# Second mixer's attention: key-by-query scores, row maxima from rounded products, division after the values

## The chip, the cores and the metric

One core of one Trainium2 chip runs the whole program in one launch. The metric is the device time of one execution in microseconds (us); three runs of the kernel before are shown, and one more execution was recorded by the profiler. Engines: TensorE (PE; its weight loads are PEld), VectorE (DVE), ScalarE (ACT), GpSimd (POOL) and SyncE (SP, here the queue that issues weight loads). Each engine works through its own list of instructions in order.

## The reference, cut to what matters

The program is a two-layer network. Layer 0 has a gated linear-attention mixer, layer 1 latent attention (the second mixer), and each layer ends in a mixture of 32 experts. The change lies in the attention of the second mixer: 16 heads, 256 queries, 512 keys (256 of the context, 256 of the sequence), 96 columns of which 32 are rotated, values of 64 columns.

```python
def softmax_attend(q, k, v):
    s = jnp.einsum('bqhd,bkhd->bhqk', q, k).astype(jnp.float32) * (MLA_QK ** -0.5)
    p = jax.nn.softmax(s, axis=-1).astype(v.dtype)
    return jnp.einsum('bhqk,bkhd->bqhd', p, v)
```

q and k are normed over their 96 columns and rotated before; the result goes through an output projection, and then to the router and the second mixture of experts.

## The kernel before, in words

`run` calls the stages in turn: `hgrn`, `moe`, `mla`, `moe`. `mla` (from line 1407 on) is the second mixer. It first projects the four token tiles (lines 1441 to 1486), and then works on four groups of four heads.

`prep(g)` (lines 1504 to 1554) makes one group ready: products for the queries (line 1512), their sum of squares (1518), inverse root (`rstd`), scaling (1520) and rotation (`rope`, 1494 to 1499), eight transposes into qT (1526); products for keys and values (1534), values copied out (1536), key sum (1541), key scaling (1544), the four rotated parts (1547), sixteen transposes into kT (1553, 1554).

`attend(g)` (lines 1557 to 1584) takes heads in pairs. For a head and each of two query tiles: a product of 128 queries by 512 keys (1567), row maximum (1569), exponential with its row sum (1572), reciprocal and scaling (1573, 1574), four transposes (1577) and a copy (1578) into PT. Then the values are multiplied (1581), and the result is split in a rounded part oH and a rest oL (1583, 1584).

The program calls `prep(0)`, and then for g = 0 to 3 `prep(g + 1)` and `attend(g)`. The adaptive weights of the layer are computed in between (`ada_piece`, line 229 on TensorE, 239 on VectorE), and GpSimd multiplies the output weights by a row of them (line 1611). In this stage a scheduler sets each engine's order when the program is built; it follows the program's text and what its model holds ready.

Two kinds of buffers tie the order down. PSUM tiles come in the order of the text out of rotations: `self.mm()` has four buffers, `self.sm()` two here. And tags with one buffer (q, sqt, kk) let a group in only when the group before has let go.

The weights of the second mixture of experts are loaded ahead by the SyncE queue into nine slots of 2 MB in the order 0, 5, 6, 2, 1, 7, 3, 4, 8 (`wload`, lines 1170 and 1173). During the mixer slot 0 holds scratch tiles, 1 the keys kTs, 2 the query weights wq, 3 and 4 the output weights, 5 wi, and 6 wkv, the weights for keys and values; a load waits until its slot is free, and those behind it wait too.

## Time and profile before

| what | value |
|---|---|
| median of three runs (lowest, highest) | 1554.08 us (1552.7, 1554.46) |
| the profiled execution, its own time | 1554.54 us |
| its span on the core | 1552.9 us |
| granted TensorE clock, mean | 0.985 of full |
| TensorE busy (matmuls) | 1474.2 us, 95% |
| VectorE busy | 808.1 us, 52% |
| ScalarE busy | 441.3 us, 28% |
| GpSimd busy | 48.9 us, 3% |
| read from memory | 498.91 MB, 322 GB/s over the span |

The busy shares are means over stages with different limits, and ends of matmuls are modelled, so 95% does not say that TensorE bounds every stage. The second mixer runs from about 894 to 1075 us of the span; its last value product ends at 1057.6. Matmuls on fp32 tiles are two instructions each in the trace (two passes), transposes and products of rounded (fp32r) tiles are one. Times in rows count from the start of the span.

### The profile page before, as it was taken

What the parts mean: (1) busy time and instruction counts of PE and PEld (TensorE: products, weight loads), DVE (VectorE), ACT (ScalarE), POOL (GpSimd) and SP (SyncE); (2) the same over time, 40 slices, a digit from 0 to 9 for tenths busy, and PEclk for the clock granted to TensorE, in tenths of its full rate; (3) what the DMA queues carried; (4) which work ended last, traced back from release to release, by engine and by line L of the source; (5) the groups of instructions that cost most, each with busy time, mean ns of one, the idle gap of its engine ahead of it and who ended that gap; (6) DMA issues with size and microseconds to landing.
All of it is one profiled execution on the core that took longest, in us unless ns stands there. A gap on an engine that the chain in (4) does not pass through costs nothing. (4 is left out here: it accounts for less than half of the span.)

```text
span 1552.9 us, 20333 instructions
## 1 busy us (share of the span) xinstructions
PE 1474.2 (95%) x8137; PEld 808.7 (52%) x8138; DVE 808.1 (52%) x1651; ACT 441.3 (28%) x937; POOL 48.9 (3%) x81
## 2 busy tenths in 40 slices
PE   7999999999799999999999988989899999999997
PEld 4677777877544444444444454447444443443433
DVE  5686748886625455355355648574333332332333
ACT  4554545663301101111011055564211111111110
POOL 0000000000000000000000103210000000000000
PEclk9999999999899999999999999999999999999999
DMA  9644444126799999999999775355799999999997
GB/s 384 272 179 179 164 189 149 62 109 232 279 364 414 429 426 428 427 427 427 428 428 422 252 301 225 137 190 204 266 417 428 427 428 428 427 428 427 428 424 263
DMA packets 63432, 501.46 MB, mean 323 GB/s; under 512 B 7008, under 2 KB 16608, under 8 KB 33120
## 3 DMA queue, kind: packets, MB, share of 16 engines
q1 hardware_dynamic: 59296, 490.87, 77.6%
q10 hardware_dynamic: 3184, 7.92, 1.5%
q0 software_dynamic: 848, 1.26, 0.3%
q8 instruction: 68, 1.11, 0.3%
q14 instruction: 36, 0.29, 0.1%
HBM read 498.91 MB, written 1.11 MB: 322 GB/s over the span
## 5 line engine op out<-in xcount | busy, mean ns | idle before, releaser
L1179 PE MATMUL mm<-w,xT 128*64 128x512 f32 x2048 | 476.8, 602 | 13.5 <-DMA w<-in_wg_dram 10.0
L1179 PEld LDWEIGHTS mm<-w,xT 128*64 128x64 f32 x2048 | 148.4, 138 | 309.6 <-issue 271.7
L1230 DVE TENSOR_TENSOR tmp<-p,rG 128x512 f32<-128x512 f32 (+1 forms) x106 | 68.0, 645 | 132.7 <-PE p L1228 132.6
L1231 DVE TENSOR_TENSOR x<-x,tmp 128x512 f32<-128x512 f32 (+1 forms) x195 | 132.5, 679 | 6.7
L1230 DVE TENSOR_TENSOR tmp<-p,x 128x512 f32<-128x512 f32 (+1 forms) x68 | 44.5, 655 | 166.3 <-PE p L1228 166.3
L1210 PE MATMUL mm<-w,x 128*64 128x512 f32 (+1 forms) x544 | 115.3, 570 | 1.4 <-ACT x L1198 1.4
L1210 PE MATMUL mm<-w,hT 128*64 128x512 f32 (+1 forms) x544 | 113.9, 570 | 1.4 <-ACT hT L1198 1.4
L560 PE MATMUL mm<-hH,wH 128*128 128x512 f32 x256 | 105.1, 410 | 0.3 <-ACT wH L289 0.3
L1029 PE MATMUL p<-sel,h2H 128*128 128x256 f32 x384 | 101.7, 300 | 2.5 <-DVE sel L1019 2.3
L562 PE MATMUL mm<-hH,wL 128*128 128x512 f32 x256 | 100.3, 392 | 0.5 <-DVE wL L291 0.5
L561 PE MATMUL mm<-hL,wH 128*128 128x512 f32 x256 | 100.0, 391 | 0.0
L1030 PE MATMUL p<-sel,h2L 128*128 128x256 f32 x384 | 98.7, 291 | 0.0
L1217 DVE SCALAR_TENSOR_TENSOR yL<-mm,wsl,yH 128x512 fp32r<-128x512 f32 (+1 forms) x68 | 48.7, 716 | 70.3 <-ACT yH L1216 70.3
L1216 ACT ACTIVATE yH<-mm,wsl 128x512 fp32r<-128x512 f32 (+1 forms) x68 | 45.1, 663 | 122.1 <-PE mm L1210 92.0
L1029 PEld LDWEIGHTS p<-sel,h2H 128*128 128x128 f32 x384 | 76.4, 200 | 5.2 <-issue 4.1
L289 ACT CAST wH<-w 128x1024 fp32r<-128x1024 f32 x55 | 57.3, 1047 | 75.7 <-PE mm L561 56.5
L1030 PEld LDWEIGHTS p<-sel,h2L 128*128 128x128 f32 x384 | 76.3, 199 | 3.1 <-DVE nblki L1098 0.8
L1227 PE MATMUL p<-yH,G 128*128 128x512 f32 (+1 forms) x174 | 76.1, 440 | 0.9 <-DVE tmp L1230 0.9
L291 DVE TENSOR_TENSOR wL<-w,wH 128x1024 fp32r<-128x1024 f32 x55 | 66.8, 1220 | 18.6 <-ACT wH L289 18.1
L1210 PEld LDWEIGHTS mm<-w,x 128*64 128x64 f32 x544 | 45.4, 137 | 58.8 <-issue 45.5
L1210 PEld LDWEIGHTS mm<-w,hT 128*64 128x64 f32 x544 | 37.5, 137 | 65.8 <-issue 59.7
L1227 PEld LDWEIGHTS p<-yH,G 128*128 128x128 f32 x174 | 32.5, 187 | 65.8 <-issue 51.5
(401 smaller groups left out, 2029.1 us busy)
## 6 DMA issues: line engine op xcount, KB each, us to landing
w<-in_wg_dram SPq DMA_DIRECT2D x52, 2048.0 KB, 16.8
w<-in_wu_dram SPq DMA_DIRECT2D x52, 2048.0 KB, 19.7
w<-in_wd_dram SPq DMA_DIRECT2D x52, 2048.0 KB, 18.7
aw<-in_ada_w_dram SPq DMA_DIRECT2D x32, 1024.0 KB, 6.5
w<-in_wd_dram SPq DMA_DIRECT2D x48, 512.0 KB, 8.8
w<-in_hg_w_dram SPq DMA_DIRECT2D x8, 2048.0 KB, 9.2
w<-in_wg_dram SPq DMA_DIRECT2D x32, 512.0 KB, 6.9
w<-in_wu_dram SPq DMA_DIRECT2D x32, 512.0 KB, 9.3
```

What stands on the lines that cost most here:

```text
L289: nc.scalar.copy(H, raw)
L291: nc.vector.tensor_tensor(L, raw, H, op=ALU.subtract)
L560: PE.matmul(p, H[:, c], hH[:, k, :], start=(k == 0), stop=False)
L561: PE.matmul(p, H[:, c], hL[:, k, :], start=False, stop=False)
L562: PE.matmul(p, L[:, c], hH[:, k, :], start=False, stop=(k == 7))
L1029: self.nc.tensor.matmul(o, self.h2H[:, tt, c], r, start=(tt == 0 and k == 0), stop=False)
L1030: self.nc.tensor.matmul(o, self.h2L[:, tt, c], r, start=False, stop=(last and k == 1))
L1179: PE.matmul(p[a * 64:(a + 1) * 64, :], xT[:, k, a * 64:(a + 1) * 64], ws[a][:, k * 512:(k + 1) * 512], start=(k == 0), stop=(k == 7))
L1210: PE.matmul(p[a * 64:(a + 1) * 64, :], hT[:, j, a * 64:(a + 1) * 64], ws[a][:, j * 1024 + n * w_:j * 1024 + n * w_ + w_], start=(j == 0), ...
L1227: PE.matmul(pc, g, yH, start=True, stop=False)
L1230: V.tensor_tensor(t, pc, rG[vec(tt)][:, ns], op=ALU.mult)
L1231: adder.tensor_tensor(x[:, tt, ns], x[:, tt, ns], t, op=ALU.add)
```

## The change

In `prep`, every query and key transpose is also copied into a rounded tile (qR, kR), eight rounded products give the scores of the group once, and their negated row maxima go into a 97th column of q. q is transposed a second time with that column into qT of 97 rows; kT gets a 97th row of ones, so that a product of kT and qT is a score less its row's maximum. In `attend`, scores are computed with keys on the partitions and queries in the columns, the exponential writes PT directly, the sums over keys are two additions on VectorE and a product with ones, and the mixed values are divided at the end. es, rs and on lie in the free end of wkv (slot 6). c becomes a part of one tile cc, in the place that kR takes later. The rest of the program is as before; behind the first edit line numbers are higher by 7 to 22.

```diff
@@ -1438,6 +1438,13 @@
             ckT = wq[:, 3584:4096]
             kg = ar.tile([128, 4, 32], F32, tag="kg", name="kg")
             skr = ar.tile([128, 4], F32, tag="skr", name="skr")
+            G.memset(kTs[96:97], 1.0)
+            cc = ar.tile([128, 4, 512], F32, tag="kR", name="cc")
+            ones = ar.tile([128, 64], F32, tag="on64", name="ones")
+            V.memset(ones, 1.0)
+
+            es = [wkv[:, c:c + 512] for c in (2496, 3008)]
+            rs, on = wkv[:, 3520:3776], wkv[:, 3776:4032]
             for tt in range(4):
                 v = 0 if tt >= 2 else 1
                 ts = slice(tt * 128, tt * 128 + 128)
@@ -1451,7 +1458,7 @@
                         self.scale(k, hT[:, tt % 2, kk, :], pt[:, k * 128:(k + 1) * 128], self.colA[1][:, kk, v:v + 1])
                 if tt == 0:
                     bw = self.mla_bias(ar)
-                jk = ar.tile([128, 4, 256], F32, tag="PT", name="jk", bufs=4)
+                jk = ar.tile([128, 4, 256], F32, tag="PT", name="jk", bufs=3)
                 S.activation(jk.rearrange("p a b -> p (a b)"), y, AF.Square, accum_out=ss[:, tt:tt + 1])
                 if tt == 0:
                     tc.keep_in_program_order(S.preload_act_table_set(TABLE))
@@ -1460,7 +1467,7 @@
                 p = self.mm()
                 for k in range(8):
                     PE.matmul(p[:, c0:416], hT[:, tt % 2, k, :], wi[:, k, c0:416], start=(k == 0), stop=(k == 7))
-                c = ar.tile([128, 512], F32, tag="pr", name="c", bufs=3)
+                c = cc[:, tt, :]
                 V.scalar_tensor_tensor(c[:, c0:416], p[:, c0:416], rx, bw[v], op0=ALU.mult, op1=ALU.add)
                 s2 = self.sp.tile([128, 2], F32, tag="s2", name="s2", bufs=4)
                 jk = ar.tile([128, 1024], F32, tag="q", name="jk")
@@ -1503,7 +1510,8 @@
 
             def prep(g):
 
-                q = ar.tile([128, 1024], F32, tag="q", name="q")[:, 0:768].rearrange("p (h e) -> p h e", h=8)
+                q = ar.tile([128, 1024], F32, tag="q", name="q")[:, 0:776].rearrange("p (h e) -> p h e", h=8)
+                q0 = q[:, :, 0:96]
                 sqt = ar.tile([128, 16, 64], F32, tag="sqt", name="sqt")
                 q2 = sqt.rearrange("p a b -> p (a b)")[:, 0:768].rearrange("p (h e) -> p h e", h=8)
                 for t in range(2):
@@ -1513,18 +1521,12 @@
                                   wq[:, k * 1536 + g * 384:k * 1536 + g * 384 + 384], start=(k == 0), stop=(k == 1))
                     pv = p[:, 0:384].rearrange("p (h e) -> p h e", h=4)
                     S.activation(q2[:, t * 4:t * 4 + 4, :], pv, AF.Square)
-                    V.tensor_tensor(q[:, t * 4:t * 4 + 4, :], pv, gq.to_broadcast([128, 4, 96]), op=ALU.mult)
+                    V.tensor_tensor(q0[:, t * 4:t * 4 + 4, :], pv, gq.to_broadcast([128, 4, 96]), op=ALU.mult)
                 sq = ar.tile([128, 8, 1], F32, tag="sq", name="sq")
                 V.tensor_reduce(sq, q2, axis=AX.X, op=ALU.add)
                 rq = self.rstd(sq[:, :, 0], 96, 8, "rsq")
-                V.tensor_tensor(q, q, rq.rearrange("p (h o) -> p h o", o=1).to_broadcast([128, 8, 96]), op=ALU.mult)
+                V.tensor_tensor(q0, q0, rq.rearrange("p (h o) -> p h o", o=1).to_broadcast([128, 8, 96]), op=ALU.mult)
                 rope(q[:, :, 64:96], cs, 8)
-                qT = ar.tile([96, 4, 256], F32, tag="qT", name="qT", bufs=2)
-                for t in range(2):
-                    pt = self.sm()
-                    for j in range(4):
-                        PE.transpose(pt[0:96, j * 128:(j + 1) * 128], q[:, t * 4 + j, :], self.ident)
-                    S.copy(qT[:, :, t * 128:(t + 1) * 128], pt[0:96].rearrange("p (j t) -> p j t", j=4))
 
                 kk = ar.tile([128, 2048], F32, tag="kk", name="kk")[:, 0:1536].rearrange("p (t h e) -> p t h e", t=4, h=4)
                 sqt = ar.tile([128, 16, 64], F32, tag="sqt", name="sqt")
@@ -1546,42 +1548,62 @@
                 for tt in range(4):
                     V.tensor_tensor(kk[:, tt, :, 64:96], rk[:, tt * 4:tt * 4 + 4].rearrange("p (h o) -> p h o", o=1).to_broadcast([128, 4, 32]),
                                     kg[:, tt:tt + 1, :].to_broadcast([128, 4, 32]), op=ALU.mult)
-                kT = kTs[0:96, g % 2]
+
+                qR = ar.tile([96, 4, 256], F32R, tag="sqt", name="qR")
+                for t in range(2):
+                    pt = self.sm()
+                    for j in range(4):
+                        PE.transpose(pt[0:96, j * 128:(j + 1) * 128], q[:, t * 4 + j, 0:96], self.ident)
+                    S.copy(qR[:, :, t * 128:(t + 1) * 128], pt[0:96].rearrange("p (j t) -> p j t", j=4))
+                kT = kTs[0:97, g % 2]
+                kR = ar.tile([96, 4, 512], F32R, tag="kR", name="kR")
                 for j in range(4):
                     pt = self.sm()
                     for tt in range(4):
                         PE.transpose(pt[0:96, tt * 128:(tt + 1) * 128], kk[:, tt, j, :], self.ident)
-                    S.copy(kT[:, j, :], pt[0:96])
+                    S.copy(kR[:, j, :], pt[0:96])
+                    S.copy(kT[0:96, j, :], pt[0:96])
+                    for t in range(2):
+                        p = self.mm()
+                        PE.matmul(p, qR[:, j, t * 128:(t + 1) * 128], kR[:, j, :], start=True, stop=True)
+                        V.tensor_reduce(q[:, t * 4 + j, 96:97], p, axis=AX.X, op=ALU.max, negate=True)
+                qT = ar.tile([97, 4, 256], F32, tag="qT", name="qT", bufs=2)
+                for t in range(2):
+                    pt = self.sm()
+                    for j in range(4):
+                        PE.transpose(pt[0:97, j * 128:(j + 1) * 128], q[:, t * 4 + j, :], self.ident)
+                    S.copy(qT[:, :, t * 128:(t + 1) * 128], pt[0:97].rearrange("p (j t) -> p j t", j=4))
                 return qT, kT, vS
 
             def attend(g, qT, kT, vS):
+
+
                 for j in range(2):
                     po = self.ac()
                     PTs = []
                     for hh in range(2):
                         h = 2 * j + hh
-                        PT = ar.tile([128, 4, 256], F32, tag="PT", name="PT", bufs=4)
+                        PT = ar.tile([128, 4, 256], F32, tag="PT", name="PT", bufs=3)
                         PTs.append(PT)
-                        for t in range(2):
+                        for b in range(2):
                             p = self.mm()
-                            PE.matmul(p, qT[:, h, t * 128:(t + 1) * 128], kT[:, h, :], start=True, stop=True)
-                            nm = ar.tile([128, 1], F32, tag="nm", name="nm", bufs=8)
-                            V.tensor_reduce(nm, p, axis=AX.X, op=ALU.max, negate=True)
-                            pr = ar.tile([128, 512], F32, tag="pr", name="pr", bufs=3)
-                            sm = ar.tile([128, 1], F32, tag="smx", name="smx", bufs=8)
-                            S.activation(pr, p, AF.Exp, bias=nm, accum_out=sm)
-                            V.reciprocal(sm, sm)
-                            V.tensor_scalar(pr, pr, sm, None, op0=ALU.mult)
-                            pt = self.sm()
-                            for c in range(4):
-                                PE.transpose(pt[:, c * 128:(c + 1) * 128], pr[:, c * 128:(c + 1) * 128], self.ident)
-                            S.copy(PT[:, :, t * 128:(t + 1) * 128], pt.rearrange("p (c q) -> p c q", c=4))
+                            for c in range(2):
+                                s = (2 * b + c) * 128
+                                PE.matmul(p[:, c * 256:(c + 1) * 256], kT[:, h, s:s + 128], qT[:, h, :], start=True, stop=True)
+                            S.activation(PT[:, 2 * b:2 * b + 2, :].rearrange("p c t -> p (c t)"), p, AF.Exp)
+                        V.tensor_tensor(es[hh], PT[:, 0:2, :].rearrange("p c t -> p (c t)"),
+                                        PT[:, 2:4, :].rearrange("p c t -> p (c t)"), op=ALU.add)
+                        V.tensor_tensor(es[hh][:, 0:256], es[hh][:, 0:256], es[hh][:, 256:512], op=ALU.add)
                     for c in range(4):
                         for hh in range(2):
                             PE.matmul(po[hh * 64:(hh + 1) * 64, 0:256], vS[:, c, 2 * j + hh, :], PTs[hh][:, c, :], start=(c == 0), stop=(c == 3))
+                    for hh in range(2):
+                        PE.matmul(po[hh * 64:(hh + 1) * 64, 256:512], ones, es[hh][:, 0:256], start=True, stop=True)
+                    V.reciprocal(rs, po[:, 256:512])
+                    V.tensor_tensor(on, po[:, 0:256], rs, op=ALU.mult)
                     o = g * 2 + j
-                    S.copy(oH[:, o, :], po[:, 0:256])
-                    V.tensor_tensor(oL[:, o, :], po[:, 0:256], oH[:, o, :], op=ALU.subtract)
+                    S.copy(oH[:, o, :], on)
+                    V.tensor_tensor(oL[:, o, :], on, oH[:, o, :], op=ALU.subtract)
 
 
             half = lambda t: [t[:, 0:2048], t[:, 2048:4096]]

```

On TensorE, at the end of attend(0) and in prep(2), the order before was this (L1534: products for keys and values; L1567: scores of attend(1); L229: adaptive weights; L1526, L1553: transposes of queries and keys).

```order
L1534 MATMUL mm<-w_3967,w_3959 128x512 x4
L1567 MATMUL mm<-w_113,qT 128x512 x4
L229 MATMUL p_8133<-w_3966,cS 32x512 x4
L1526 MATMUL p_7857<-ident,q 96x128 x4
L1526 MATMUL p_7863<-ident,q 96x128 x4
L1567 MATMUL mm<-w_113,qT 128x512
L229 MATMUL p_8133<-w_3966,cS 32x512 x3
L229 MATMUL p_8133<-w_112,cS 32x512
L1567 MATMUL mm<-w_113,qT 128x512 x2
L1553 MATMUL p_7908<-ident,kk 96x128 x4
L1553 MATMUL p_7914<-ident,kk 96x128 x4
```

After the change the same place begins with the products with ones of attend(0) (L1601); L1520, L1536, L1556 are the former L1512, L1534, L1526.

```order
L1601 MATMUL p_7800<-w_3967,ones 64x256 x2
L1520 MATMUL mm<-w_3959 128x384 x4
L1536 MATMUL mm<-w_3967,w_3959 128x512 x4
L229 MATMUL p_8115<-w_3966,cS 32x512 x7
L229 MATMUL p_8115<-w_112,cS 32x512 x4
L1556 MATMUL p_7908<-ident,q 96x128 x4
L1556 MATMUL p_7914<-ident,q 96x128 x4
```

And some rows on, at the end of prep(2), with the rounded products (L1568), the second transposes of the queries (L1574) and the first scores of attend(1) (L1592):

```order
L1563 MATMUL p_7960<-ident,kk 96x128 x4
L1568 MATMUL mm<-kR,qR 128x512 x2
L1574 MATMUL p_7974<-ident,q 97x128 x2
L1568 MATMUL mm<-kR,qR 128x512 x2
L1574 MATMUL p_7980<-ident,q 97x128 x2
L1574 MATMUL p_7974<-ident,q 97x128
L1592 MATMUL mm<-qT,w_113 128x256 x2
L1574 MATMUL p_7980<-ident,q 97x128
L1592 MATMUL mm<-qT,w_113 128x256
```

Scores of attend(1) stood ahead of the transposes of prep(2), and stand now behind its rounded products and among its last transposes.

On VectorE, at the end of the rotation of group 0, before (L1499 rotation, L1542 key sum, L1518 sum of squares of group 1):

```order
L1498 TENSOR_TENSOR q<-q,rp_7489 128x8x2x8
L1499 TENSOR_TENSOR q<-q,rp_7488 128x8x2x8
L1542 TENSOR_TENSOR sk<-sk,skr 128x16
L1518 TENSOR_REDUCE sq<-sqt 128x8
L166 TENSOR_SCALAR rsm<-sk 128x16
```

After (L1506 and L1544 are the former L1499 and L1542; L239 is the sum for the adaptive weights):

```order
L1505 TENSOR_TENSOR q<-q,rp_7489 128x8x2x8
L1506 TENSOR_TENSOR q<-q,rp_7488 128x8x2x8
L1544 TENSOR_TENSOR sk<-sk,skr 128x16
L239 TENSOR_TENSOR w_112<-p_8061,w_112 128x512
L166 TENSOR_SCALAR rsm<-sk 128x16
L171 TENSOR_TENSOR rsm<-rsm,rsr 128x16
```

The sum of line 239 stood 26 instructions further on, behind work of group 1, and no work of group 1 stands here now.

On the SyncE queue, the loads for the second mixture of experts, before (w_3966 is slot 5, w_112 slot 0, w_3967 slot 6, w_3959 slot 2, w_3964 and w_3965 slots 3 and 4, w_113 slot 1):

```order
L1170 DMA w_3966<-in_wg_dram 128x4096
L1170 DMA w_112<-in_wg_dram 128x4096
L1170 DMA w_3967<-in_wu_dram 128x4096
L1170 DMA w_3959<-in_wu_dram 128x4096
L1173 DMA w_3964<-in_wg_dram 128x1024 x2
L1170 DMA w_113<-in_wd_dram 128x4096
L1173 DMA w_3964<-in_wg_dram 128x1024 x2
L1173 DMA w_3965<-in_wg_dram 128x1024 x4
```

After:

```order
L1170 DMA w_3966<-in_wg_dram 128x4096
L1170 DMA w_3959<-in_wu_dram 128x4096
L1170 DMA w_112<-in_wg_dram 128x4096
L1173 DMA w_3964<-in_wg_dram 128x1024 x2
L1170 DMA w_113<-in_wd_dram 128x4096
L1170 DMA w_3967<-in_wu_dram 128x4096
L1173 DMA w_3965<-in_wg_dram 128x1024 x2
```

The load into slot 6 went from the third place to behind the load into slot 1, which waits for the last scores.

## Rows read from the trace of the kernel before

**Rows 1.** Stretches: us, busy (x) per engine, TensorE clock, transfer share, GB/s.
```profile
945.00:1057.60 112.60, 102.55 (x516) 52.34 (x514) 74.24 (x176) 62.78 (x155) 28.83 (x19) 0.98 0.49 184
...
1057.60:1094.00 36.40, 29.41 (x156) 25.14 (x156) 22.33 (x66) 15.22 (x30) 1.75 (x7) 0.87 0.63 216
...
1122.00:1300.00 178.00, 175.32 (x834) 74.30 (x830) 61.41 (x108) 29.06 (x54) 0.00 (x0) 0.99 1.01 423
```

**Rows 2.** SyncE's weight queue, waits 890 to 1200: us in total, times, longest.
```profile
SPq L1170 <- PE mm L1179: 27.5, 4, 9.2
...
SPq L1170 <- PE mm L1567: 20.0, 1, 20.0
```

**Rows 3.** Chain of waits in the mixer: start us, us, engine, line, count.
```profile
931.14 2.58 PE mm L1512 x8
...
935.44 0.87 PE p L1526 x8
...
978.78 3.44 PE mm L1567 x8
...
1030.76 3.03 PE p L1581 x14
...
1055.75 1.87 PE p L1581 x14
...
1061.29 0.93 PE mm L1630 x4
```

**Rows 4.** Groups by shape, 919 to 1060: count, busy us, mean ns, idle before.
```profile
L1574 DVE TENSOR_SCALAR pr<-pr,smx 128x512 f32<-128x512 f32 x32 | 25.7, 812 | 1.5
...
L1569 DVE TENSOR_REDUCE nm<-mm 128x1 f32<-128x512 f32 x32 | 21.5, 682 | 3.0 <-PE mm L1567 2.8
...
L1572 ACT ACTIVATE pr<-mm,nm 128x512 f32<-128x512 f32 x32 | 22.1, 695 | 3.5 <-DVE nm L1569 3.3
...
L1554 ACT COPY w<-p 96x512 f32<-96x512 f32 x16 | 8.5, 583 | 9.4 <-PE p L1553 5.5 <-DMA w<-in_ada_b_dram 3.9
...
L1573 DVE RECIPROCAL smx<-smx 128x1 f32<-128x1 f32 x32 | 4.8, 156 | 15.6 <-ACT pr L1572 15.6
```

**Rows 5.** Groups, whole span, VectorE, same columns.
```profile
L391 DVE RECIPROCAL mx<-mx 128x16 f32<-128x16 f32 x1 | 0.3, 252 | 0.0
```

**Rows 6.** Order of time, VectorE, preparation of group 0: start us, us, instruction.
```profile
928.74 0.94 DVE L1518 TENSOR_REDUCE sq<-sqt 128x8 f32<-128x768 f32 x1
...
934.72 0.17 DVE L1542 TENSOR_TENSOR sk<-sk,skr 128x16 f32<-128x16 f32 x1
...
937.66 1.21 DVE L1544 TENSOR_TENSOR kk<-kk,rsr 128x1024 f32<-128x1024 f32 x1
...
938.80 0.89 DVE L1547 TENSOR_TENSOR kk<-rsr,kg 128x128 f32<-128x128 f32 x4
```

**Rows 7.** Order of time, ScalarE and its queue.
```profile
945.00 0.33 ACTq L233 DMA_DIRECT2D w<-in_ada_b_dram  x1
...
952.97 0.58 ACT L1554 COPY w<-p 96x512 f32<-96x512 f32 x1 [3.90 <-DMA w<-in_ada_b_dram]
```

**Rows 8.** Order of time, VectorE and GpSimd (POOL).
```profile
890.11 0.72 DVE L1231 TENSOR_TENSOR x<-x,tmp 128x256 f32<-128x256 f32 x1
...
891.20 0.43 DVE L1231 TENSOR_TENSOR x<-x,tmp 128x256 f32<-128x256 f32 x1
...
944.00 0.69 DVE L239 TENSOR_TENSOR w<-p,w 128x512 f32<-128x512 f32 x1
...
957.84 19.45 POOL L1611 TENSOR_TENSOR w<-w,x 128x1024 f32<-128x1024 f32 x8 [4.47 <-PE p L229]
...
958.41 2.07 DVE L1574 TENSOR_SCALAR pr<-pr,smx 128x512 f32<-128x512 f32 x1
...
1029.29 0.49 DVE L1574 TENSOR_SCALAR pr<-pr,smx 128x512 f32<-128x512 f32 x1
```

**Rows 9.** Stretch behind a wait, columns as in Rows 1.
```profile
1028.00:1036.00 8.00, 7.27 (x50) 4.45 (x50) 3.99 (x11) 3.89 (x10) 0.30 (x1) 0.79 0.34 115
```

## The prediction

> **What bounds the kernel now.** I read the totals first (the table above), then stretches, then the chain of waits inside the stretch that the change touches. The reader is to see two regimes.
>
> From 1122 us on the transfers set the pace: 423 GB/s with the transfer engines busy all the time [rows 1]. These are the expert weights of the second mixture of experts. In the mixer itself the transfers run at 184 GB/s, and at 216 GB/s in the 36 us behind it [rows 1]: the weight queue does not lack bandwidth there, it lacks free slots. Its waits name who holds them: the last scores of the mixer (20.0 us for the slot of the keys) and the first expert products (27.5 us) [rows 2]. Both stand behind the attention. So whatever the mixer gains or loses moves the point at which the transfers saturate, and the end of the kernel by as much. Time in the mixer counts one for one.
>
> Inside the mixer TensorE is the bound for most of 920 to 1057.6 us. The chain there runs through projections, scores and transposes with hardly a gap, each at a steady price per instruction [rows 3]. It can do so because the preparation of group g+1 (its sums of squares, rotations and transposes) lies beside the scores and transposes of group g. The question for the change is therefore less what it saves than whether this overlap stays.
>
> **The change, engine by engine.** TensorE: 32 score products leave, two passes of 0.43 us each [rows 3], 27.5 us; the 64 half-width products that replace them have half the columns per pass, 0.215 us, again 27.5. 128 transposes of probabilities leave at 0.11 us, 14.0; 32 transposes of queries come, 3.5; 32 rounded products come at the 0.23 us of one rounded 512-column pass, 7.4; 16 products with ones at the 0.134 us of a value-product pass, 4.3 [rows 3]. Sum: 42.7 added, 41.5 removed. TensorE is even.
>
> VectorE: 32 scalings (25.7 us as they ran) and 32 narrow reciprocals (4.8) leave, the 32 maxima stay [rows 4]. 16 sums of 512 columns come, taken at the 0.68 of a 512-column maximum [rows 4], and 16 of 256 at 0.43 [rows 8], 17.8 us; 8 products of 256 (0.43), 3.4; and 8 reciprocals of 256 columns, which no row shows. Below they cannot cost less than a 256-column product, 0.43; above, the step from 0.156 us at 1 column to 0.252 at 16 [rows 4, 5] gives 6.4 ns a column, 1.8 us. I take 1.8, since it is the same operation. Together 36 us for 30: no saving either. They lie beside the value products and cost nothing as long as TensorE has those to run.
>
> ScalarE: 32 copies of transposed probabilities and 32 readings of the accumulated sums leave, 24 copies of the 0.583 us kind come [rows 4]; it is not the bound. Costed at nothing: the single-row memset on GpSimd, which is busy for 3% of the span, the memset of ones, the merged c tile and the third PT buffer (the code never holds more than three at once before their products).
>
> **What moves decides.** The row maxima of group g+1 now take eight tiles of the same four-buffer rotation from which the scores of group g are taken next. The first scores of group g can therefore not start before the fifth maximum of g+1 is read. The order above shows it: queries, keys, maxima and second transposes of prep(2) stand in one block, and only among its last transposes come the scores of attend(1); where before 4 scores stood between the projections and the query transposes, there are now eleven adaptive-weight products at most, and none in the last group. Preparation and attention go one after the other, and each waiting step of the preparation is in the open.
>
> Its steps, from the first group of before, which ran without other work in front of it: from the sum of squares of q (928.74) to the key sum (934.72) 6.0 us; then 0.1, the inverse root of 16 columns (2.9 us there with work of the next group inside, as the order above shows; I take half, 1.4), the key scaling 1.15 and the four rope parts 0.85 [rows 6]: 9.5 us. Then the new part: transposes and their copy 1.0, product 0.4, eight maxima of 0.68 [rows 4]: 7.2 with the waits between (ScalarE's eight copies of 0.583, 4.7 us, lie under it). Attention: eight half products for a pair of heads 3.44, the last exponential 0.70 and its signals 0.95, sixteen value passes 2.14, four passes of ones 0.53: 7.06, twice 14.1; after a preparation 13.1, since some scores stand among its transposes.
>
> **The sum**, on the clock of the profiled execution. Keys of group 0 are ready at 938.5 (938.8 + 0.9 before, less what of group 1 lay in front). +7.2 for maxima, and +3 because ScalarE waits there: before, the second of two issues of the ada_b load kept it idle for 3.9 us, up to 952.97, until the first, of 945.0, had landed [rows 7], and in the new order the copies of the last two heads stand behind that issue. The q tile is free at 949. Group 1: 1.4 for the two gain products, 9.5: 959.9. Here GpSimd comes in. Its eight products on the output weights run 19.45 us in one piece and start 13.8 us after the sum of line 239 [rows 8]; that sum stands now right behind the rotation of group 0, at about 935, so they run from 949 to 968, over the preparation of group 1. A VectorE sum of two SBUF tiles took 0.72 us beside a GpSimd product and 0.43 after it [rows 8]: it waits until the other is done. Group 1 has over fifteen such steps in a row. Of the 19.45 us I estimate some 6 to pass under steps that do not read two SBUF tiles (the gain products, the two sums, the copies of the values) and under waits for ScalarE: +13, with bounds of 0 and 19.4. 972.9; maxima 980.1; attend(0) 993.2. Two more rounds of 4.0 (query products 2.58 [rows 3], last square, gain) + 9.5 + 7.2 + 13.1 = 33.8: 1060.8. attend(3) 14.1 and 0.7 for the router: 1075.6. Nine of the output projection's passes lay before 1057.6 and come now after, 2.1: 1077.7. Against 1057.6 that is **+20.1 us**: 1554.54 + 20.1, about 1575. The profiled execution is 0.5 us above the median of the three runs, so the same holds for the median.
>
> The first half of the up-projection weights of expert pair 0 now waits for the end of attention (slot 6 holds the sums). 2 MB at 423 GB/s are 5 us in a stretch with half its bandwidth free [rows 1], and they are wanted only after the router: nothing. The load of the second output weights stands now behind four more loads of adaptive weights; their slots come free by about 945, and GpSimd wants those weights for its fifth product, at about 959: nothing.
>
> **The clock.** Behind a wait for VectorE TensorE's granted clock was 0.79 of full for 8 us, a mixture of its two levels of 1.2 and 2.4 GHz, and 14 value passes took 3.03 us instead of 1.87 [rows 9, 3]; the dip cost 0.21 x 8 = 1.7 us. I keep one such dip on both sides, so the sum stays 1575. The Trainium skill, TensorE: Matmul & The Clock Gate, section HAM oscillation — how this bites in real kernels, tells of bursts of matmuls separated by waits that lose the clock in every round; by that rule the second rival holds, and the time is 1587.
>
> **Rivals.**
> *Overlap kept (faster).* The VectorE stalls that TensorE waited for were mainly its scalings, which GpSimd held to about 2 us each (2.07 us in [rows 8] against 0.49 alone). They leave, and the sums that replace them are not waited for by the value products. If the preparation's steps fitted beside TensorE's work, some 7 us of waits would go and 1.2 us of work come: 1549. The 7 us are what TensorE waited longer than it had to behind four scalings of the 2 us kind. It decides if TensorE is idle for under 2 us in a preparation. Against it: 9.5 + 7.2 = 16.7 us of steps in a row stand against some 12 us of TensorE work in the same preparation (query products 2.58, key and value products 3.44 as eight passes of 0.43, 32 transposes of 0.11, rounded products 1.9).
> *Clock lost in each round.* A preparation has two waits of TensorE, one before the query and key transposes and one among the maxima. If a dip of 1.7 us followed each, four preparations would have eight, seven more than in the sum: 12 us, 1587. For: these waits come at regular intervals. Against: over the whole mixer the clock was 0.98 [rows 1] though waits stood in it too.
> *Weight stream absorbs it (same).* If the transfers had slack left behind 1122 us, the mixer's loss would vanish: 1555. Against: 423 GB/s without a break.
> *Not what it says.* If the rounded products ran at the pace of full ones, 0.86 instead of 0.23, 20 us of TensorE work would come, half of it under the maxima: 1585. Rows of rounded passes speak against it.
>
> **Numbers.** The forecast has 0.66. Its own range is 1558 to 1590: without the GpSimd wait and the ada_b wait the sum is 20.1 - 16, so 1559; with a full GpSimd wait and half of the dips it is 20.1 + 6.4 + 6, so 1587, and a few us are left for what I did not see. The clock lost in each round has 0.13, slow rounded products 0.04, the overlap kept 0.10, the loss absorbed 0.07. A measurement of this kernel tells 0.2%, 3 us, from no change. So slower has 0.66 + 0.13 + 0.04 = 0.83, within 0.2% 0.07, faster 0.10. The range 1558 to 1590 holds the forecast and most of the two cases above it; it leaves out the faster and the unchanged case, 0.17.
>
> **What would show it.** After: TensorE idle 6 to 9 us in each preparation, released by VectorE; scores of attend(g) only after the maxima of prep(g+1); VectorE steps of 2 us beside GpSimd in group 1; last value product near 1077; from there to the end the same time as now, about 495 us; reciprocals of 256 columns near 1.8 us. Wrong if the scores of attend(0) start before 965, or if the last value product comes before 1058.

## The result, and the profile after

| what | before | changed |
|---|---|---|
| median, same chip, four runs each | 1553.39 us (1551.62 to 1554.46) | 1574.24 us (1573.6 to 1575.27) |
| ratio, 95% interval | 1 | 1.0126 [1.0113, 1.0140] |
| span of the profiled execution | 1552.9 us | 1573.5 us |
| mixer: TensorE's clock from 945 us on | 0.98 [rows 1] | 0.87 |

The change costs 1.26%, some 20 us. The forecast was 1575. The medians by themselves are 20.9 us apart; the ratio on record is 19.6 us of 1554, and differences below are taken from ratios.

The three stretches that answer to [rows 1], in the profile of the changed kernel (busy us per engine, then clock, transfer share, GB/s); the mixer is cut at the first product of the output projection.

```profile
945.00:1075.70 130.70, 109.87 (x549) 70.83 (x549) 94.49 (x175) 57.38 (x125) 26.88 (x16) 0.87 0.33 122
1075.70:1112.00 36.30, 29.31 (x154) 24.62 (x155) 22.35 (x55) 14.79 (x29) 1.46 (x5) 0.91 0.84 309
1142.00:1300.00 158.00, 157.41 (x756) 68.23 (x752) 56.61 (x99) 26.03 (x48) 0.00 (x0) 1.00 1.01 422
```

The expert stage is what it was. From the output projection to the end it is 1573.5 - 1075.7 = 497.8 us, before 1552.9 - 1057.6 = 495.3. So 18.1 us lie in the mixer and 2.5 behind it, and nothing there gives any back. From 945 us to the output projection TensorE is busy 109.9 of 130.7 us and stands still for 21; before it stood still for 10 of 112.6 [rows 1]. Of the 18.1 us, 10.8 are thus more standing still, and 7.3 are more busy time, in a stretch with the lower granted clock.

TensorE's waits from 920 us to the output projection, by what released it (us in total, times, longest):

```profile
PE p L1556 <- DVE sk L1544: 9.9, 1, 9.9
PE p L1563 <- DVE kk L1549: 5.9, 4, 2.3
PE p L1556 <- DVE q L1506: 5.1, 3, 3.7
PE mm L1568 <- ACT kR L1564: 2.6, 3, 2.1
```

L1556 and L1563 are the first transposes of queries and keys. So 20.9 us are waits for VectorE in a preparation: 2.5 for group 0 (ahead of 945 us), 10.8, 3.0 and 4.7 for the others. Before, TensorE waited for VectorE mainly in the attention, for the scalings of probabilities and their reciprocals:

```profile
PE p L1577 <- DVE pr L1574: 5.0, 3, 1.9
PE p L1577 <- DVE smx L1573: 1.9, 2, 1.3
```

TensorE in the order of time, through the preparation of group 2 and half of attend(1) (start us, us, instruction, [idle before it]):

```profile
993.89 2.85 PE L1520 MATMUL mm<-w 128*128 128x384 f32 x8
996.57 3.60 PE L1536 MATMUL mm<-w,w 128*128 128x512 f32 x8
1000.10 2.78 PE L229 MATMUL p<-w,cS 128*32 128x512 f32 x22
1004.09 1.08 PE L1556 MATMUL p<-ident,q 128*96 128x128 f32 x8 [1.22 <-DVE q L1506]
1006.95 1.91 PE L1563 MATMUL p<-ident,kk 128*96 128x128 f32 x8 [1.77 <-DVE kk L1549]
1009.10 1.22 PE L1568 MATMUL mm<-kR,qR 96*128 96x512 f32 x2 [0.24 <-ACT kR L1564]
...
1014.46 1.03 PE L1592 MATMUL mm<-qT,w 97*128 97x256 f32 x4
...
1018.35 1.95 PE L1599 MATMUL p<-PT,vS 128*64 128x256 f32 x16
```

No score of attend(1) (L1592) stands before 1014.46. In front of it are the key transposes, eight in 1.91 us where the query transposes took 1.08, and rounded products at 1.22 us a pair: from 1006.9 to 1012.5 us, behind two waits, the granted clock is 0.50, the lower of its two levels. Only 2.8 us of adaptive products (L229) help to fill the preparation. Of its 20.6 us TensorE stands still for 3.2; the rest is its own work, part of it at half pace.

VectorE in the preparation of group 1, with GpSimd's row, and two steps of group 2:

```profile
948.62 19.21 POOL L1633 TENSOR_TENSOR w<-w,x 128x1024 f32<-128x1024 f32 x8 [4.43 <-DMA x<-adad]
...
954.08 0.94 DVE L1526 TENSOR_REDUCE sq<-sqt 128x8 f32<-128x768 f32 x1
...
955.86 2.06 DVE L171 TENSOR_TENSOR rsm<-rsm,rsr 128x8 f32<-128x8 f32 x1
...
958.18 2.05 DVE L172 TENSOR_TENSOR rsm<-rsm,rsr 128x8 f32<-128x8 f32 x1
...
960.27 2.26 DVE L173 SCALAR_TENSOR_TENSOR rsr<-rsm,rsr 128x8 f32<-128x8 f32 x1
...
962.79 2.84 DVE L1528 TENSOR_TENSOR q<-q,rsr 128x768 f32<-128x768 f32 x1
...
971.47 0.89 DVE L1549 TENSOR_TENSOR kk<-rsr,kg 128x128 f32<-128x128 f32 x4
...
1000.11 0.16 DVE L172 TENSOR_TENSOR rsm<-rsm,rsr 128x8 f32<-128x8 f32 x1
...
1000.74 0.96 DVE L1528 TENSOR_TENSOR q<-q,rsr 128x768 f32<-128x768 f32 x1
```

A product of eight columns (L172) takes 2.05 us beside GpSimd and 0.16 without. From the first sum (954.08) to the last key part (972.4) the chain took 18.3 us in group 1, and 9.3 in group 2.

The groups that answer to [rows 4, 5], by shape:

```profile
L1602 DVE RECIPROCAL w<-p 128x256 f32<-128x256 f32 x8 | 14.1, 1758 | 5.9 <-PE p L1601 5.9
L1594 DVE TENSOR_TENSOR w<-PT 128x512 f32<-128x512 f32 x16 | 12.9, 804 | 10.6 <-ACT PT L1593 10.4
L1569 DVE TENSOR_REDUCE q<-mm 128x1 f32<-128x512 f32 x32 | 20.2, 685 | 15.6 <-PE mm L1568 15.6
...
L1568 PE MATMUL mm<-kR,qR 96*128 96x512 f32 x32 | 14.0, 533 | 2.6 <-ACT kR L1564 2.6
```

### The profile page after: what moved, and what is told of

It reads as the page before. It is cut to its first block, busy times and chain, and to the rows that moved or that the text cites. A ratio compares the mean times of both kernels' runs of the same rounds, so it can differ in the third digit from the quotient of the medians.

```text
span 1573.5 us, 20319 instructions
## 1 busy us (share of the span) xinstructions
PE 1478.6 (94%) x8169; PEld 825.5 (52%) x8170; DVE 826.7 (53%) x1636; ACT 432.5 (27%) x897; POOL 52.6 (3%) x82
## 3 DMA queue, kind: packets, MB, share of 16 engines
q0 software_dynamic: 848, 1.26, 0.3%
## 5 line engine op out<-in xcount | busy, mean ns | idle before, releaser
L560 PE MATMUL mm<-hH,wH 128*128 128x512 f32 x256 | 105.1, 410 | 0.3 <-ACT wH L289 0.3
L291 DVE TENSOR_TENSOR wL<-w,wH 128x1024 fp32r<-128x1024 f32 x55 | 66.9, 1222 | 19.0 <-ACT wH L289 18.1
```

The source lines that it names most:

```text
L291: nc.vector.tensor_tensor(L, raw, H, op=ALU.subtract)
L560: PE.matmul(p, H[:, c], hH[:, k, :], start=(k == 0), stop=False)
```

## The experiments

Theory 1 is the prediction's: a preparation no longer lies beside the attention, and its steps on VectorE (with GpSimd's hold in group 1) are what TensorE waits for. The rivals: GpSimd alone, the clock, TensorE's own work, or the division and the sums in place of the maxima. Differences between kernels are taken from the ratios to the kernel before that ran on the same chip; a thousandth is 1.55 us. By the intervals such a difference is uncertain by some 3 to 4 us, which is why the traces are read beside it.

| run | median us | ratio [95%] |
|---|---|---|
| max_other_banks | 1576.35 | 1.0130 [1.0109, 1.0152] |
| no_gpsimd_products | 1563.13 | 1.0053 [1.0034, 1.0073] |
| before_no_gpsimd_products | 1549.12 | 0.9958 [0.9942, 0.9974] |
| one_bias_load | 1572.87 | 1.0109 [1.0089, 1.0128] |
| other_banks_no_gpsimd | 1559.77 | 1.0033 [1.0021, 1.0045] |
| split_order | 1561.12 | 1.0045 [1.0025, 1.0064] |
| clock_filler | 1573.25 | 1.0119 [1.0099, 1.0139] |
| clock_filler_short | 1571.2 | 1.0101 [1.0083, 1.0119] |
| no_maxima | 1543.17 | 0.9929 [0.9911, 0.9947] |
| before_no_maxima | 1552.58 | 0.9985 [0.9973, 0.9997] |
| split_gate_after | 1546.49 | 0.9952 [0.9936, 0.9969] |
| before_gate_after | 1549.4 | 0.9970 [0.9957, 0.9984] |

**The shared rotation.**

```diff
-                        p = self.mm()
+                        p = self.sm()
                         PE.matmul(p, qR[:, j, t * 128:(t + 1) * 128], kR[:, j, :], start=True, stop=True)
```

> The changed kernel, with one word edited: the eight rounded products of a preparation go to the two banks that serve the transposes instead of the four-buffer rotation from which the scores are taken. Nothing else is edited; TensorE's instructions then fall into another order, with the scores of attend(g) among the transposes and maxima of prep(g+1). Theory 1 (the shared rotation puts preparation and attention one after the other): the 9.5 us of VectorE steps of each preparation go under the attention again, a round costs 24 to 28 us instead of 33 to 35, and 15 to 25 us of the 20.9 come back: 1549 to 1559. Rival A (the time went into GpSimd's hold on VectorE and the second load of biases, which order doesn't touch): 1570 to 1575. Rival B (the clock: each waiting stretch halves it and this stays): under half comes back, 1565 to 1572.

Nothing came back, and the time lies above all three ranges, though the order did change: TensorE's list now has scores between transposes and rounded products, as scores stood among the transposes before the change. Stretches of this kernel, the last two in the changed kernel, and this kernel's longest wait of TensorE:

```profile
945.00:980.00 35.00, 16.77 (x55) 7.70 (x55) 25.12 (x26) 8.84 (x22) 21.88 (x13) 0.71 0.46 179
980.00:1020.00 40.00, 40.00 (x201) 24.86 (x200) 30.96 (x68) 20.61 (x48) 0.00 (x0) 0.96 0.14 53
1020.00:1060.00 40.00, 39.88 (x224) 21.32 (x223) 30.06 (x67) 18.86 (x42) 2.08 (x4) 1.00 0.54 211
```

```profile
980.00:1020.00 40.00, 36.76 (x193) 24.69 (x193) 27.81 (x58) 18.82 (x42) 0.00 (x0) 0.91 0.20 78
1020.00:1060.00 40.00, 34.63 (x164) 23.78 (x162) 30.85 (x61) 20.14 (x43) 7.46 (x7) 0.87 0.35 132
```

```profile
PE p L1556 <- DVE q L1506: 12.5, 1, 12.5
```

From 980 us on TensorE stands still for 0.1 of 80 us (8.6 in the changed kernel): there the overlap is back. It was lost ahead of that. Order of time, second transposes of group 0 in the changed kernel, and then in this one, with two value passes and the output projection:

```profile
947.73 0.83 PE L1574 MATMUL p<-ident,q 128*97 128x128 f32 x5
```

```profile
957.00 1.17 PE L1574 MATMUL p<-ident,q 128*97 128x128 f32 x4 [0.30 <-DVE q L1569]
...
994.37 0.65 PE L1599 MATMUL p<-PT,vS 128*64 128x256 f32 x2
994.95 0.74 PE L1568 MATMUL p<-kR,qR 96*128 96x512 f32 x2
...
1077.64 0.50 PE L1652 MATMUL mm<-partH,oH 128*128 128x512 f32 x1
```

The preparation of group 0 came to its second transposes 9.3 us late: its maxima and key transposes now take turns on two banks, and ScalarE's wait for the biases (4.3 us) stands in front of the last of the key tiles. From there to the projection (1075.62 in the changed kernel) it is 120.6 us for 127.9, in spite of the 12.5 us that the next query transposes waited for VectorE beside GpSimd. So the edit moved the loss, and does not price the rotation by itself.

The two value passes show a cost that the prediction had left out: 0.58 us to the next start, where sixteen in a row take 1.78 (1018.35 to 1020.13 in the changed kernel's trace, the product with ones begins there), 0.22 for two. So the change from value passes to other work takes 0.36 us here, and an interleaved order has more of them; how much of the gain they ate was not measured. The Trainium skill, TensorEngine Tiling (Array Packing), section Key Properties, says that a change of tiling drains TensorE. The row agrees: the value passes are 128 by 64, and the rounded product behind them takes the whole width.

**The same without GpSimd.** The line above, and the eight products left out.

> The rounded products on the transposes' two banks, as in max_other_banks, and without GpSimd's eight products (left out). max_other_banks alone gained nothing: its rounds behind 980 us ran without a wait of TensorE, but as long as those of the changed kernel, and its first round lost 12.5 us at one wait for VectorE beside GpSimd. Theory 1 (in max_other_banks GpSimd's hold only ate the gain): without GpSimd the overlapped order beats the serial one, by the 8.6 us that TensorE idles from 980 to 1060 in the changed kernel: 1553 to 1557 against 1563. Theory 2 (TensorE is the bound in either order, and what the overlap saves in waits it loses in switches between scores, transposes and value passes): no better than no_gpsimd_products, 1560 to 1566.

1.0033 against the 1.0053 of no_gpsimd_products: 3.1 us, with intervals that overlap, and a median at the edge of the second theory's range: the times do not show a gain. Order of time, the same two places:

```profile
957.55 1.17 PE L1574 MATMUL p<-ident,q 128*97 128x128 f32 x4 [0.30 <-DVE q L1569]
...
1062.69 0.50 PE L1650 MATMUL mm<-partH,oH 128*128 128x512 f32 x1
```

105.1 us from the second transposes of group 0 to the projection; in no_gpsimd_products they are 948.02 to 1063.73, 115.7. Of these 10.6 us some 4 are products of group 1 that here lay ahead of 957 (all for the queries, half of those for keys and values: 2.6 + 1.7). The other 6 are what the overlapping rounds gain. Group 0 is 9.5 us later; less the same 4 of products, it loses over 5, so nearly as much.

**GpSimd's products.**

```diff
-                    for j in range(8):
-                        G.tensor_tensor(wo_(j), wo_(j), gm, op=ALU.mult)
```

> The changed kernel without GpSimd's eight products of the output weights with the gate row (left out, nothing takes their place). Theory 1: GpSimd's 19.2 us lie over the preparation of group 1, which took 18.3 us from its first sum to its last key part against 9.3 in group 2; without them 9 us go, 1565. Rival A (most of the loss is GpSimd's hold): 15 us or more go, 1559 or less. Rival B (TensorE would have waited there anyway): under 3 us go, 1571 or more.

> The control: the kernel before without the same eight products. There they ran beside scalings of the probabilities, four of which took about 2 us each and made TensorE wait some 7 us longer. Theory 1: 5 to 8 us go, 1546 to 1549, so the products alone cost the change only 1 to 4 us more than they cost before. Rival A (they cost the kernel before nothing): 1553.

In the changed kernel they cost 0.0073 x 1554 = 11.3 us, before 6.5. So of the 19.6 us some 5 are GpSimd's, a difference hardly larger than its uncertainty; the rest stays. VectorE in group 1 without them, first sum and last key part:

```profile
952.68 0.94 DVE L1526 TENSOR_REDUCE sq<-sqt 128x8 f32<-128x768 f32 x1
...
961.22 0.89 DVE L1549 TENSOR_TENSOR kk<-rsr,kg 128x128 f32<-128x128 f32 x4
```

9.4 us for 18.3.

**One load of the biases.**

```diff
-        if k == 5 or (l == 1 and g and k == 7):
+        if k == 5:
```

> The changed kernel with the load of the adaptive biases issued once, at the sixth piece, and not again at the eighth. Theory 1: ScalarE's wait of 2.7 to 3.6 us for the landing of the first issue, in front of the copies of the last keys of group 0, goes, and everything behind moves by as much: 1571. Rival A (the wait is covered by GpSimd's hold on the next preparation, which starts at its own time): no difference, 1574.

ScalarE, in the changed kernel and then in this one:

```profile
945.56 0.58 ACT L1564 CAST kR<-p 96x512 fp32r<-96x512 f32 x1 [3.60 <-DMA w<-in_ada_b_dram]
```

```profile
943.40 0.58 ACT L1564 CAST kR<-p 96x512 fp32r<-96x512 f32 x1 [2.31 <-PE p L1563]
```

The third copy of a key tile comes 2.2 us sooner, of which 0.9 were there before it (the first copy is at 939.05 for 939.92), so the load cost it 1.3 us; without the load it waits for TensorE instead. The ratio gives 2.6 us, with intervals that overlap: the trace fits theory 1, and the times can't tell it from nothing.

**The preparation cut in two.**

```diff
-            def prep(g):
+            def prep_a(g):
...
+                return q, kk, vS
+
+            def prep_b(g, q, kk, vS):
                 qR = ar.tile([96, 4, 256], F32R, tag="sqt", name="qR")
...
-                    ready.append(prep(g + 1))
+                    nxt = prep_a(g + 1)
...
-                attend(g, *ready[g])
+                attend(g, *ready)
+                if g < 3:
+                    ready = prep_b(g + 1, *nxt)
```

> The changed kernel with the preparation cut in two: projections, norms and rotation of group g+1 stand ahead of attend(g), its transposes, rounded products and maxima behind it. Scores and value passes stay in one piece, TensorE changes its kind of work as seldom as in the changed kernel, but the chain of 9.5 us on VectorE lies beside the attention. Theory 1 (the chain in the open costs): the waits of TensorE before the query and key transposes go (21 us in all, 10.8 of them in group 1), GpSimd's hold falls on the sums of attend(0) instead and takes some of it back: 1558 to 1566. Theory 2 (TensorE's own work is the bound): 1570 to 1575. Rival A (the sums of attend(g) now queue behind the chain on VectorE and the value products wait): slower, 1576 to 1582.

12.6 us came back, within the range of theory 1. TensorE's waits from 920 to 1062 us:

```profile
PE mm L1595 <- ACT kk L1540: 4.2, 2, 3.5
PE p L1604 <- DVE w L1599: 3.7, 1, 3.7
PE p L1566 <- DVE kk L1549: 2.3, 1, 2.3
```

The waits before the transposes are down to 2.5 us. The two that are new lie in attend(0) beside GpSimd, as expected, and together they are 8 us for the 10 of TensorE's longest wait before. Where the waits are gone the clock is up too: 1.00 for 0.91 and 0.87 from 980 to 1060 us, so the 12.6 us hold what the clock costs, which the next runs estimate.

**The clock.** Products that nobody reads fill the waits.

```diff
+                fp = self.ac()
+                for i in range((0, 18, 3, 8)[g]):
+                    PE.matmul(fp[:, 0:256], self.ident, vS[:, 3].rearrange("p a b -> p (a b)"), start=True, stop=True)
...
+                for i in range((0, 1, 2, 1)[g]):
+                    PE.matmul(fp[:, 0:384], self.ident, q[:, 0:4, 0:96], start=True, stop=True)
```

> The changed kernel with products that nobody reads put into TensorE's waits of each preparation (18, 3 and 8 passes of 256 columns before the query transposes of groups 1, 2 and 3, and 1, 2 and 1 products of 384 columns before the key transposes), so that it hardly stands still there. Theory 1 (the waits also cost clock: key transposes 1.91 for 0.95 us, rounded products 1.2 for 0.73 a pair): the granted clock of 980 to 1060 goes from 0.89 to 0.97 or more, and 4 to 8 us come back, 1566 to 1570. Rival A (the copies of ScalarE and the maxima set that stretch, not the clock): the clock rises but the time stays, 1573 to 1575. Rival B (the filler itself delays the transposes): slower, 1576 or more.

> clock_filler with the filler of group 1 cut to fit its wait. In clock_filler the rounds of groups 2 and 3 were 0.5 and 2.0 us shorter than in the changed kernel, at a granted clock of 1.00 for 0.89, and group 1 went from its query transposes to the first scores in 8.2 us for 12.3, but there the filler ran past the end of the wait and held the query transposes back until 975.2 for 969.1. Now 20 products of 256 columns stand there, on the squares that ScalarE writes, which VectorE does not hold back. Theory 1 (the clock costs some 2 us a round beside the wait itself): 1567 to 1571. Rival A (the round is set by VectorE and ScalarE whatever the clock): 1573 to 1575.

The first gained 1 us (rival A), the second 3.9 by the ratios, just outside the range of theory 1; both have intervals that overlap the changed kernel's. Stretches of the second, and its key transposes and first rounded products in group 2:

```profile
980.00:1020.00 40.00, 40.00 (x218) 24.95 (x212) 28.94 (x61) 20.12 (x45) 0.00 (x0) 1.00 0.33 125
1020.00:1060.00 40.00, 37.52 (x199) 25.48 (x196) 32.07 (x63) 20.17 (x43) 7.43 (x7) 1.00 0.36 133
```

```profile
1008.78 1.08 PE L1570 MATMUL p<-ident,kk 128*96 128x128 f32 x8
...
1010.78 0.73 PE L1575 MATMUL mm<-kR,qR 96*128 96x512 f32 x2
```

The clock is 1.00 for 80 us, the transposes take 1.08 for 1.91 and a rounded pair 0.73 for 1.22, and still the rounds of groups 2 and 3, from the end of one attention to the end of the next, are 32.3 and 33.1 us for 33.1 and 35.1. By these rows the clock's price is some 3 us in two rounds, less than the slower passes add up to; that ScalarE's copies and the maxima hide the rest fits, but is not shown. Group 1 gave no answer in either run: the filler held the query transposes back by 5 to 6 us (974.2 and 975.3 for 969.1). From there to the first scores it then was 8.2 us for 12.3 in both, but the keys were ready by then, so what the low clock costs there stays open.

**The maxima, or the division.** In no_maxima the rounded products, the maxima and the second transposes are left out, in before_no_maxima line 1569; both scale the scores inside the exponential.

```diff
-                    S.copy(kR[:, j, :], pt[0:96])
...
-                    for t in range(2):
-                        p = self.mm()
-                        PE.matmul(p, qR[:, j, t * 128:(t + 1) * 128], kR[:, j, :], start=True, stop=True)
-                        V.tensor_reduce(q[:, t * 4 + j, 96:97], p, axis=AX.X, op=ALU.max, negate=True)
...
-                            S.activation(PT[:, 2 * b:2 * b + 2, :].rearrange("p c t -> p (c t)"), p, AF.Exp)
+                            S.activation(PT[:, 2 * b:2 * b + 2, :].rearrange("p c t -> p (c t)"), p, AF.Exp, scale=0.015625)
```

> The changed kernel without maxima: the rounded products, the row maxima, the second transposes of the queries and the 97th row are left out, and the scores are scaled by 1/64 inside the exponential so that it stays finite. Sums by the product with ones, the reciprocals and the division stay. Theory 1: four preparations lose 7.2 us each, and nothing takes the score buffers ahead of attend(g): 1540 to 1547, less than the kernel before; so the part that costs is the maxima, not the sums and the division. Rival A (reciprocals and division are the cost, since they stand between the value products of one pair and the next): 1560 or more.

> The control for no_maxima: the kernel before without its 32 row maxima (left out; the scores are scaled by 1/64 inside the exponential instead). Theory 1 (before, the maxima lay beside TensorE's work and cost little): 1547 to 1553; then sums by ones, division behind and half-width scores by themselves gain the difference to the 1543.2 of no_maxima, 4 to 10 us, and the maxima from rounded products lose some 30. Rival A (the maxima cost the kernel before as much as the new part gains): 1543 or less, and the sums and the division gain nothing.

Both came as theory 1 has it, and the pair takes the change apart. Maxima in the changed kernel, with all that they need there and the order that they force: 0.0197 x 1554 = 30.6 us. Maxima before: 2.3, they lay beside TensorE's work. What is left without maxima on either side, half-width scores, sums by ones and division behind the values, is 0.0056 faster, 8.7 us. 30.6 - 2.3 - 8.7 = 19.6 is the change; this follows from how the three are taken and is no test of them. One part of the change gains, and the other takes that three times over.

**A version that beats both.** The order of split_order and the single load, and GpSimd's products replaced by four of VectorE behind the output projection; the control has the last alone.

```diff
+                V.tensor_tensor(acc[tt][n], acc[tt][n], x[:, 1, ns], op=ALU.mult)
                 V.tensor_tensor(x[:, tt, ns], x[:, tt, ns], acc[tt][n], op=ALU.add)
```

> A version put together from what paid: the order of split_order, one load of the biases, and the gate row applied behind the output projection (four VectorE products of 512 columns on the accumulated sums, in place of GpSimd's eight on the weights). Theory 1 (the three are nearly independent): 1561.1, less 6 to 11 for GpSimd's hold, less 1.4 for the load, plus up to 2.7 for the four products of 0.68 us: 1549 to 1555, level with the kernel before or faster. Rival A (in split_order GpSimd's hold was hidden, so only the products' cost is left): 1560 to 1563.

> The control: the kernel before with the gate row applied behind the output projection in the same way. Theory 1: the 1549.1 without the products plus 0 to 2.7 for the four new ones: 1549 to 1552; so what split_gate_after gains over the kernel before comes from the gate and not from the new attention. Rival A (the four products stand on the chain behind the projection at full length and more): 1553 or more.

0.9952 and 0.9970. Both beat the kernel before, the first by more than was expected. The new attention, cut in two, is 2.8 us better than the old with the same gate, with intervals that overlap, and it has the single load as well, which the control lacks and which was never tried in the kernel before. So that its loss of 20 us is undone is shown; that it gains is not. Stretches of split_gate_after:

```profile
945.00:980.00 35.00, 35.00 (x180) 20.66 (x178) 27.44 (x62) 18.45 (x45) 0.00 (x0) 1.00 0.51 189
980.00:1020.00 40.00, 39.92 (x215) 25.01 (x215) 33.69 (x82) 21.12 (x51) 2.05 (x4) 1.00 0.42 152
```

TensorE waits for 0.08 us in 75, at full clock: what is left in this stretch is its own work.

## Why the prediction was right

- **One for one.** The mixer's end moved from 1057.6 to 1075.7 us (+18.1, predicted 1075.6), and from there to the end it took 2.5 us more, near the 2.1 predicted for the projection's passes that no longer interleave. That 1075.6 was met to 0.1 us is luck, as the steps below show: the order was right, and errors of several us cancelled.
- **Preparation and attention one after the other.** So it ran, and with the slow chain of the preparation laid beside the attention 12.6 us came back. But one sign did not come: TensorE was to stand still for 6 to 9 us in each preparation, and it was 2.5, 10.8, 3.0 and 4.7 us. More of the chain than thought lay under TensorE's own work, which took longer than the sum had it. The four-buffer rotation, named as the cause, does set the order: with it freed the scores moved among the maxima, and without GpSimd the rounds gained some 6 us. That run lost nearly as much in group 0, so the rotation's own price stays open; that of the missing overlap does not.
- **GpSimd, +13 of 0 to 19.4.** The chain of group 1 grew by 9.0 us in the trace; taking the products away gave 11.3, but the kernel before paid 6.5 for them too, in scalings that the change removed. So of the change itself GpSimd accounts for some 5 us; the 13 of the sum stand for the whole hold, since the old end time that it is compared with has the 6.5 in it.
- **Steps.** Key parts of group 0 ended at 939.5 (938.5). The first gain product of group 1 came at 952.5 (949): it waited for the second transposes to be done with the q tile, to which the sum had given no time, and they ran in turn with query products at a granted clock of 0.72 (947 to 953). Without GpSimd, at full pace, it came at 951.1. The +3 for the second load was too much, since its removal brought the copy 1.3 us forward. The lateness of 3.5 and the hold that was 4 too large cancelled: keys of group 1 ready at 972.4 (972.9). attend(0) ended at 993.9 (993.2), the rounds took 33.1 and 35.1 (33.8), attend(3) 13.5 (14.8 with the router).
- **Attention.** The five terms for a pair of heads add up to 7.76 as written, not 7.06, which holds only if the 0.95 of signals has the 0.70 of the exponential in it. Measured are 6.2 us a pair (1069.45 to 1075.62): the sixteen value passes start 3.65 us after the scores, and nothing waits for the last exponential.
- **Prices.** The reciprocal of 256 columns took 1758 ns: 1.8 from two narrow ones was right. Rounded products came to 0.44 us each (14.0 for 32), not 0.23: they run in pairs among other work, many at half clock. The sums of 512 columns took 804 ns for 680; two of the sixteen were held (1.18 and 2.00 us) while GpSimd worked.
- **The clock.** Here the sum was wrong: one dip was kept on both sides, and every round had them (0.87 for 0.98). Its price was some 3 us in the two rounds where it was measured, and is open in group 1; the 12 us of the rival did not show: all busy time in the mixer grew by 7.3. The Trainium skill, TensorE: Matmul & The Clock Gate, section HAM oscillation — how this bites in real kernels, tells of waits between bursts that lose the clock in every round. The trace agrees: 0.76, 0.91 and 0.87 from 945, 980 and 1020 us on.
- **Rivals.** *Overlap kept* is refuted by the order of the rows, *weight stream absorbs it* by the 2.5 us more behind the mixer, where it would have been 18 less, and *not what it says* by 0.73 us for a pair of rounded products at full clock, where it had 0.86 for one.

## What to carry to other kernels

When a step that needs a result of the whole row moves from the consumer to the producer, ask what the consumer does meanwhile: the 32 maxima cost 2 us beside TensorE's work, and 31 in front of it, with the rounded products and second transposes that they need there. Cut a preparation where its slow chain ends, and lay a block of the other engine's work over the chain. Two changes in one can hide each other: take one out of both kernels, and see what the other does by itself. And a sum that is met to 0.1 us is no proof of its terms: read each of them in the trace.

## What was not expected

A two-input VectorE step of 128 by 8 was held as long as one of 128 by 768: 2.05 us beside GpSimd for 0.16 alone, and 2.84 for 0.96, both 1.9 us more; so a chain of small steps suffers most. TensorE paid 0.36 us to go from two value passes to other work. And its clock mattered little in the two rounds where that was tried: eight key transposes took 1.91 us for 1.08, and a whole round 0.9 to 2.0 us more.
